# Norm between two blocks of a Trainium2 kernel: the row factor through a matrix of ones

## The chip, the cores and the metric

The kernel runs on one core of one Trainium2 chip. The core has five engines with instruction queues of their own: TensorE (PE, matrix products into PSUM), VectorE (DVE), ScalarE (ACT, functions out of tables), GpSimd (POOL) and SyncE (SP, which here only starts transfers). They run at the same time and wait for each other through semaphores. The metric is the device time of one execution in microseconds (us); lower is better.

## What is computed

The reference runs two transformer blocks one after the other on 256 rows of 2048 columns, all in fp32. The first block normalises its input, runs a sliding-window attention with sinks, gates it, multiplies by `w_out_a`, and adds the normalised product to its input. The second block normalises that sum and goes on with two attention branches and a feed-forward part. What matters here is the seam:

```python
y = (o * silu(z)) @ w_out_a                 # (256, 2048)
x = x + rmsnorm(y, g_post)                  # end of the first block
h = rmsnorm(x, attn_norm_g_2)               # start of the second
proj = h @ w_in_2
# rmsnorm(y, g) = y * rsqrt(mean(y*y over the 2048 columns) + 1e-6) * g
```

So each of the 256 rows of y needs one factor, the reciprocal root of the mean of its squares. No row of x can be had before the last column of y is known.

## The kernel before

**Layout.** In this part the kernel holds everything transposed: a tile has 128 of the 2048 columns of the model in its partitions and the 256 rows of the sequence along its free axis. Sixteen such tiles make y. A sum over the model's columns is therefore a sum over partitions and over sixteen tiles, and the factor that comes out must stand as a row of 256 numbers in every partition, to be multiplied with the tiles.

**Products.** A product with weights is made of three parts in reduced fp32 (`F32R`): each weight is split by ACT into a high part `w_hi` (line 85) and by DVE into the rest `w_lo` (line 86), and the activations likewise (`split_scaled`, lines 248 and 249). All matrix products are issued by the helper `mm`, line 209. Products of plain fp32, as those with the tile `ones` (a 128x128 matrix of ones, line 215), show up as two passes each in the trace.

**The stage around the change.** The loop at line 663 makes blocks 0 to 14 of `out_a`. For each, `total` adds two halves of a PSUM bank (ACT copy line 417, DVE add line 212) into a half of a tile `y`, `sq.add` squares it (ACT, line 265) and adds the square to the accumulator `sq.acc` (DVE, line 212), and line 667 scales `y` by the gain. Block 15 is made by `gemm_sum` (line 358), which sums all three parts into one PSUM region; its square (`sq.last`) is taken from PSUM and kept apart from the accumulator (`urgent=True`).

Then follows the norm. `sq.sums` (line 271) takes both squares, 128 rows of the sequence at a time, as the stationary operand against one column of `ones`: four products that give the 256 sums as two columns of 128 partitions. `rstd` (line 281) makes the mean plus epsilon on DVE (line 285) and raises it to the power -0.5 on POOL (line 290, exponent tile `mhalf`). `rows` (line 293) puts the 256 factors on two diagonals (DVE, line 297) and multiplies them by `ones`, which gives the row of factors in every partition, in PSUM. `residual_1` (line 688) multiplies a tile of y by that row (line 691) and adds x (line 692); `second_h` (line 695) splits the result for the next products, `in_2`. Both are issued tile by tile as `in_2` asks for them.

**What sets the order.** The program is written with a tile framework. Each engine works through its instructions in a fixed order, which a planner decides when the kernel is built, from its own estimates of when each input is ready; the order of the code only decides between instructions that are ready. Instructions marked by `pin` (in `residual_1` and `second_h`) keep the order of the code among each other. Tiles come from pools with a fixed number of slots (`unit`: 57 tiles of 128x512; PSUM banks with tag `t`: two), and an instruction that writes a new tile waits for a free slot.

`busy(n, cols)` (line 352) issues n products of the first gated tile with itself, of which nobody reads the result. They take up PE between real products.

**ACT's tables.** A function of ACT needs its table loaded. Before the change the trace has three loads, at lines 232, 1055 (Silu) and 1110 (Sqrt, at the end).

Of the kernel before, what the change touches and what calls it, by code (L numbers as in the profile page):

```python
# [9 lines left out]
F32 = mybir.dt.float32  # L10
F32R = mybir.dt.float32r
AF = mybir.ActivationFunctionType
ALU = mybir.AluOpType

P = 128
S = 256
D = 2048
# [3 lines left out]
EPS = 1e-6  # L21
# [150 lines left out]
def block_kernel(ctx, tc, order, w, x01, xt, bc, rw, cst, out):  # L172
    nc = tc.nc
    const = ctx.enter_context(tc.tile_pool(name="const", bufs=1))
# [12 lines left out]
    def unit(name, dt=F32):  # L187
        return up.tile([P, 512], dt, name=name, tag="u", bufs=NU)
# [7 lines left out]
    def sm(name, n=4):  # L196
        return small.tile([P, n], F32, name=name, tag="sm", bufs=16)

    def bank(tag):
        return psum.tile([P, 512], F32, name=f"ps_{tag}", tag=tag, bufs={"g": 4, "s": 2, "t": 2}[tag])  # L200

    def half(t, i):
        return t[:, (i % 2) * S:(i % 2) * S + S]
# [4 lines left out]
    def mm(o, a, b, start, stop):  # L208
        nc.tensor.matmul(out=o, lhsT=a, rhs=b, start=start, stop=stop, skip_group_check=True)  # L209
# [5 lines left out]
    ones = const.tile([P, P], F32, name="ones")  # L215
# [12 lines left out]
    warm = psum.tile([P, 512], F32, name="ps_warm", tag="t", bufs=2)  # L228
    for i in range(13):
        nc.tensor.matmul(out=warm[:, 0:P], lhsT=ones, rhs=ones, start=True, stop=True, skip_group_check=True)  # L230
    mhalf = const.tile([P, 4], F32, name="mhalf")
    nc.scalar.activation(out=mhalf, in_=ones[:, 0:4], func=AF.Copy, scale=-0.5)
    ident = const.tile([P, P], F32, name="ident")
# [3 lines left out]
    def gcol(base, i):  # L237
        return colt[:, base + i:base + i + 1]
# [42 lines left out]
    def rstd(src, dim, scale=None):  # L281
        n = src.shape[-1]
        t = sm("ms", n)
        if scale is None:
            nc.vector.tensor_scalar(out=t, in0=src, scalar1=1.0 / dim, scalar2=EPS, op0=ALU.mult, op1=ALU.add)  # L285
        else:
            nc.vector.scalar_tensor_tensor(out=t, in0=src, scalar=1.0 / dim, in1=scale, op0=ALU.mult, op1=ALU.mult)
            nc.vector.tensor_scalar(out=t, in0=t, scalar1=EPS, scalar2=None, op0=ALU.add)
        r = sm("rstd", n)
        nc.gpsimd.tensor_tensor(out=r, in0=t, in1=mhalf[:, 0:n], op=ALU.pow)  # L290
        return r

    def rows(r, rb=None):

        dg = unit("diag")[:, 0:S]
        for tb in range(2):
            nc.vector.tensor_scalar(out=dg[:, tb * P:tb * P + P], in0=ident, scalar1=r[:, tb:tb + 1], scalar2=None,
                                    op0=ALU.mult)
        ps = bank("t")
        mm(ps[:, 0:S], ones, dg, True, True)  # L300
        if rb is not None:
            nc.vector.tensor_copy(out=rb, in_=ps[:, 0:S])
        return ps[:, 0:S]
# [48 lines left out]
    def busy(n, cols):  # L352

        ps = bank("s")
        for _ in range(n):
            mm(ps[:, 0:cols], g[0][:, 0:P], g[0][:, 0:cols], True, True)

    def gemm_sum(name, m, acts):

        kind[0] = "hi"  # L360
        ps = bank("g")
        n = len(acts)
        for k in range(n):
            hi, lo = W.take(name, k * P, m * P)
            mm(ps[:, 0:S], hi, acts[k][:, 0:S], k == 0, False)
            mm(ps[:, 0:S], hi, acts[k][:, S:], False, False)
            mm(ps[:, 0:S], lo, acts[k][:, 0:S], False, k == n - 1)
            between.tiles(1)
        return ps

    def blocks(name, m0, n, acts):

        for j, ps in enumerate(gemm4(name, range(m0, m0 + 4), acts)):
            yield j, ps
        for j in range(4, n):
            yield j, gemm(name, m0 + j, acts)
# [38 lines left out]
    def total(o, ps):  # L415

        nc.scalar.copy(out=o, in_=ps[:, S:])
        tt(o, o, ps[:, 0:S], ALU.add)
# [75 lines left out]
    sq = Squares(8)  # L494
# [30 lines left out]
    rb = unit("rb_a")[:, 0:S]  # L525
# [134 lines left out]
    sq = Squares(16, urgent=True)  # L660
    y2 = [unit("y") for _ in range(8)]
    n_next = len(W.order) + KD * KD
    for m, ps in blocks("out_a", 0, 15, g):
        t = half(y2[m // 2], m)
        total(t, ps)
        sq.add(t)
        nc.scalar.activation(out=t, in_=t, func=AF.Copy, scale=gcol(G_POST, m))
        y.append(t)
        if m in (5, 8, 11):
            W.cut(len(W.order))  # L670
            W.cut(len(W.order) + HALF)
            for i in range(2):
                W.cut(n_next + (m - 5) // 3 * CH + i * HALF,
                      [(unit("w_hi_u", F32R), unit("w_lo_u", F32R)) for _ in range(2)])
    ps = gemm_sum("out_a", 15, g)
    sq.add(ps[:, 0:S])
    sums = sq.sums()
    busy(8, P)
    r = rstd(sums, D)
    busy(2, S)  # L680
    rb = rows(r)
    busy(8, 512)
    t = half(y2[7], 1)
    nc.scalar.activation(out=t, in_=ps[:, 0:S], func=AF.Copy, scale=gcol(G_POST, 15))
# [143 lines left out]
    for u in range(4):  # L828
# [12 lines left out]
        for tb in range(2):  # L841
            t = unit("v_m")
# [162 lines left out]
    for i in range(4):  # L1005
        parts = []
        for tb, ps in enumerate(gemm_nat("diff", i * 512, y_d)):
            t = gates[i][tb]
# [67 lines left out]
    for cb in range(3):  # L1076
        for tb, ps in enumerate(gemm_nat("down", cb * 512, act)):
            residual(cb, tb, ps)
            t = x2n[2 * cb + tb]
# [18 lines left out]
    for tb in range(2):  # L1098
# [3 lines left out]
        for i, (cols, ps) in enumerate(parts):  # L1102
# [3 lines left out]
            if i + 1 < len(parts):  # L1106
                nc.vector.scalar_tensor_tensor(out=ms3[:, tb:tb + 1], in0=tot[:, 5 * tb + 3:5 * tb + 4],
                                               scalar=1.0 / D, in1=ms3[:, tb:tb + 1], op0=ALU.mult, op1=ALU.add)
        r = sm("rms", 1)
        nc.scalar.activation(out=r, in_=tot[:, 5 * tb + 2 + len(parts):5 * tb + 3 + len(parts)], func=AF.Sqrt,  # L1110
                             scale=1.0 / D, bias=ms3[:, tb:tb + 1])
        nc.vector.reciprocal(out=r, in_=r)  # L1112
        for cb in range(4):
            t = x2n[2 * cb + tb]
# [110 lines left out]
```

## Time and profile before

| | us |
|---|---|
| median of 3 runs | 1979.8 (1979.0 to 1981.18) |
| the profiled execution, its own time | 1978.53 |
| its span, first to last instruction | 1976.8 |
| last product of block 15 issued | 329.14 |
| squares of block 15 start on ACT | 329.46 |
| first `y` times the row factor on DVE | 332.88 |
| first product of `in_2` | 335.00 |

The times inside the execution count from the start of its span. [...] A name as `ps_t<-ones,sq` reads: the tile written, then the tiles read. PE is the execution of products, PEld the load of their stationary operand. The times of single products are modelled at their ends.

### The profile page before, as it was taken

What the parts mean: (1) busy time and instruction counts of PE and PEld (TensorE: products, weight loads), DVE (VectorE), ACT (ScalarE), POOL (GpSimd) and SP (SyncE); (2) the same over time, 40 slices, a digit from 0 to 9 for tenths busy, and PEclk for the clock granted to TensorE, in tenths of its full rate; (3) what the DMA queues carried; (4) which work ended last, traced back from release to release, by engine and by line L of the source; (5) the groups of instructions that cost most, each with busy time, mean ns of one, the idle gap of its engine ahead of it and who ended that gap; (6) DMA issues with size and microseconds to landing.
All of it is one profiled execution on the core that took longest, in us unless ns stands there. A gap on an engine that the chain in (4) does not pass through costs nothing. (4 is left out here: it accounts for less than half of the span.)

```text
span 1976.8 us, 27209 instructions
## 1 busy us (share of the span) xinstructions
PE 1961.3 (99%) x9756; PEld 1648.6 (83%) x9756; DVE 1246.6 (63%) x1960; ACT 1000.3 (51%) x1580; POOL 524.8 (27%) x1067
## 2 busy tenths in 40 slices
PE   9999999999999999999999999999999999999998
PEld 8888888888888888888888888887888888888887
DVE  7889766888856655566666666655555555545553
ACT  6677664755645444455554444544444444444443
POOL 0555200022401300013143575433444333330000
PEclk9999999999999999999999999999999999999999
DMA  8565554455555555555556665655656556565553
GB/s 304 186 210 192 187 208 164 171 177 175 174 187 195 173 220 226 198 182 181 204 202 228 212 216 186 241 204 199 207 206 206 204 208 210 206 226 192 192 191 107
DMA packets 100793, 393.16 MB, mean 199 GB/s; under 512 B 27248, under 2 KB 53104, under 8 KB 57520
## 3 DMA queue, kind: packets, MB, share of 16 engines
q1 hardware_dynamic: 65184, 366.17, 52.1%
q0 software_dynamic: 34320, 23.27, 4.2%
q10 hardware_dynamic: 1152, 1.97, 0.3%
q8 instruction: 77, 1.26, 0.3%
q14 instruction: 60, 0.49, 0.1%
HBM read 364.03 MB, written 2.10 MB: 185 GB/s over the span
## 5 line engine op out<-in xcount | busy, mean ns | idle before, releaser
L86 DVE TENSOR_TENSOR w_lo<-w_raw,w_hi 128x1024 fp32r<-128x1024 f32 (+1 forms) x677 | 820.8, 1217 | 555.6 <-ACT w_hi L85 550.7
L85 ACT CAST w_hi<-w_raw 128x1024 fp32r<-128x1024 f32 (+1 forms) x677 | 706.6, 1048 | 699.4 <-PE ps_g L209 632.1
L209 PE MATMUL ps_g<-w_lo,t_hi 128*128 128x512 f32 x1176 | 457.6, 389 | 0.8 <-DVE w_lo L86 0.8
L209 PE MATMUL ps_g<-w_hi,t_hi 128*128 128x512 f32 x1176 | 457.6, 389 | 0.3 <-ACT w_hi L85 0.3
L209 PE MATMUL ps_g<-w_hi,t_lo 128*128 128x512 f32 x1176 | 457.3, 389 | 0.0
L452 POOL DMA_DIRECT2D turned<-turn x576 | 281.7, 497 | 393.2 <-DVE turn L459 169.6
L209 PE MATMUL ps_g<-h,w_hi 128*128 128x512 f32 x1160 | 283.7, 393 | 1.9 <-ACT w_hi L85 1.8
L452 POOL DMA_DIRECT2D prob_t<-prob_tr x336 | 164.5, 498 | 400.6 <-DVE prob_tr L467 249.6
L209 PEld LDWEIGHTS ps_g<-w_lo,t_hi 128*128 128x128 f32 x1176 | 220.7, 188 | 47.0 <-DVE w_lo L86 1.1
L209 PEld LDWEIGHTS ps_g<-w_hi,t_hi 128*128 128x128 f32 x1176 | 220.7, 188 | 46.7 <-ACT w_hi L85 0.7
L209 PEld LDWEIGHTS ps_g<-w_hi,t_lo 128*128 128x128 f32 x1176 | 220.7, 188 | 45.6
L209 PEld LDWEIGHTS ps_g<-h,w_hi 128*128 128x128 f32 x1160 | 212.0, 188 | 46.6 <-issue 2.7
L209 PE MATMUL ps_g<-w_hi,h 128*128 128x512 f32 x768 | 240.9, 391 | 0.0
L209 PEld LDWEIGHTS ps_g<-w_hi,h 128*128 128x128 f32 x768 | 144.2, 188 | 29.8
L209 PEld LDWEIGHTS ps_g<-h,w_lo 128*128 128x128 f32 x1160 | 150.2, 191 | 9.9 <-issue 3.0
L209 PE MATMUL ps_g<-h,w_lo 128*128 128x256 f32 x1160 | 155.1, 284 | 0.0
L209 PE MATMUL ps_g<-w_lo,h 128*128 128x512 f32 x384 | 149.7, 390 | 0.8 <-DVE w_lo L86 0.8
L290 POOL TENSOR_TENSOR rstd<-ms,mhalf 128x2 f32<-128x2 f32 (+1 forms) x10 | 8.4, 837 | 354.5 <-DVE ms L285 338.8
L209 PEld LDWEIGHTS ps_g<-w_lo,h 128*128 128x128 f32 x384 | 72.1, 188 | 16.2 <-DVE w_lo L86 1.6
L452 POOL DMA_DIRECT2D o_t<-o_tr x128 | 62.8, 498 | 63.5 <-issue 24.9
L209 PE MATMUL ps_g<-w_hi,y_m 128*128 128x512 f32 x256 | 79.5, 389 | 0.0
L209 PE MATMUL ps_g<-w_hi,y_d 128*128 128x512 f32 x256 | 79.0, 389 | 0.0
(242 smaller groups left out, 1800.8 us busy)
## 6 DMA issues: line engine op xcount, KB each, us to landing
w_raw<-w SPq DMA_DIRECT2D x337, 1024.0 KB, 5.0
turned<-turn POOLq DMA_DIRECT2D x576, 16.0 KB, 3.9
prob_t<-prob_tr POOLq DMA_DIRECT2D x336, 24.0 KB, 3.6
row<-rw POOLq DMA_DIRECT2D x12, 256.0 KB, 4.0
prob_t<-prob_tr SPq DMA_DIRECT2D x112, 24.0 KB, 2.9
w_raw<-w SPq DMA_DIRECT2D x5, 512.0 KB, 7.5
x1n<-turn SPq DMA_DIRECT2D x128, 16.0 KB, 1.8
o_t<-o_tr POOLq DMA_DIRECT2D x128, 16.0 KB, 3.9
```

What stands on the lines that cost most here:

```text
L85: a = nc.scalar.copy(out=hi[:, q], in_=src[:, q])
L86: b = nc.vector.tensor_tensor(out=lo[:, q], in0=src[:, q], in1=hi.bitcast(F32)[:, q], op=ALU.subtract)
L209: nc.tensor.matmul(out=o, lhsT=a, rhs=b, start=start, stop=stop, skip_group_check=True)
L290: nc.gpsimd.tensor_tensor(out=r, in0=t, in1=mhalf[:, 0:n], op=ALU.pow)
L452: (fourth if fourth and a == 3 else queue).dma_start(out=o[32 * b:32 * b + 32, a * n:a * n + n], in_=tr[32 * a:32 * a + 32, b * n:b * n + n])
```

## The change

The row factor is made in another way. The product takes the matrix of ones as the stationary operand and the squares as the moving one, 256 columns wide, so each product gives the sums as a row in every partition at once: one for the accumulated squares of blocks 0 to 14, written ahead of block 15's products, and one for block 15's own squares behind them, into the same PSUM region. ACT then takes the root of sums / 2048 + epsilon into an SBUF tile `rb_y`, with epsilon from a new tile of one column, and DVE takes the reciprocal of all 256 columns in place. The mean on DVE, the power on POOL, the two diagonals and the second product with ones go away here (`sums`, `rstd` and `rows` stay for the other norms). Between the two products of ones, a Sqrt of the accumulated squares into `rb_y` is written, whose result is overwritten later. The fillers behind the norm become `busy(4, P)` and `busy(8, 512)`, where they were `busy(8, P)`, `busy(2, S)` and `busy(8, 512)`.

```diff
@@ -228,6 +228,8 @@
     for i in range(13):
         nc.tensor.matmul(out=warm[:, 0:P], lhsT=ones, rhs=ones, start=True, stop=True, skip_group_check=True)
+    eps = const.tile([P, 1], F32, name="eps")
+    nc.vector.memset(eps, EPS)
     mhalf = const.tile([P, 4], F32, name="mhalf")
@@ -672,13 +674,17 @@
+    rb = unit("rb_y")[:, 0:S]
+    sums = bank("t")[:, 0:S]
+    mm(sums, ones, sq.acc, True, False)
+    nc.scalar.activation(out=rb, in_=sq.acc, func=AF.Sqrt)
     ps = gemm_sum("out_a", 15, g)
     sq.add(ps[:, 0:S])
-    sums = sq.sums()
-    busy(8, P)
-    r = rstd(sums, D)
-    busy(2, S)
-    rb = rows(r)
+    mm(sums, ones, sq.last, False, True)
+    busy(4, P)
+    nc.scalar.activation(out=rb, in_=sums, func=AF.Sqrt, scale=1.0 / D, bias=eps)
+    nc.vector.reciprocal(out=rb, in_=rb)
     busy(8, 512)
     t = half(y2[7], 1)
     nc.scalar.activation(out=t, in_=ps[:, 0:S], func=AF.Copy, scale=gcol(G_POST, 15))
```

## The prediction

> **What bounds the kernel now.** I began with the profile's page, which has TensorE (PE) at work for 99% of the span, so anything that holds PE up goes into the total.
>
> ```profile
> span 1976.8 us, 27209 instructions
> PE 1961.3 (99%) x9756; PEld 1648.6 (83%) x9756; DVE 1246.6 (63%) x1960; ACT 1000.3 (51%) x1580; POOL 524.8 (27%) x1067
> ```
>
> Next I took the busy time in the stretch of the norm and in the one behind it (columns: stretch, its length, busy time of PE, weight load, DVE, ACT and POOL, granted clock).
>
> ```profile
> 329.50:335.00 5.50, 4.54 (x27) 3.61 (x26) 2.69 (x9) 1.63 (x4) 0.71 (x1) 1.00 0.27 85
> 335.00:360.00 25.00, 25.00 (x143) 21.96 (x144) 23.33 (x49) 13.35 (x23) 0.00 (x0) 1.00 0.22 85
> ```
>
> From 335.00 us PE has no free time, so a later start there is not made up again. In the norm PE looks busy (4.54 of 5.50 us), but its own timeline shows with what: everything called ps_s is filler from busy(), whose result nobody reads. (Columns: start, duration, engine, line, what; in brackets the idle time before it.)
>
> ```profile
> 329.14 0.28 PE L209 MATMUL ps_g<-g,w_lo 128*128 128x256 f32 x1
> 329.26 0.50 PE L209 MATMUL ps_t<-ones,sq 128*128 128x1 f32 x4
> 329.62 0.42 PE L209 MATMUL ps_s<-g 128*128 128x128 f32 x2
> 329.90 0.61 PE L209 MATMUL ps_t<-ones,sq 128*128 128x1 f32 x4
> 330.36 1.15 PE L209 MATMUL ps_s<-g 128*128 128x128 f32 x8
> 332.14 0.70 PE L209 MATMUL ps_t<-diag,ones 128*128 128x256 f32 x2 [0.63 <-DVE diag L297]
> 332.49 2.18 PE L209 MATMUL ps_s<-g 128*128 128x512 f32 x8
> 335.00 0.50 PE L209 MATMUL ps_g<-h,w_hi_u 128*128 128x512 f32 x1 [0.34 <-DVE h L249]
> ```
>
> So the real limit is the chain from the last product of block 15 (its end is 329.14 + 0.28 = 329.42) to the first product of the next stage at 335.00. The timelines of DVE and of ACT fill it in.
>
> ```profile
> 324.11 0.42 DVE L212 TENSOR_TENSOR y<-y,ps_g 128x256 f32<-128x256 f32 x1 [3.06 <-ACT y L417]
> 325.02 0.42 DVE L212 TENSOR_TENSOR sq<-sq 128x256 f32<-128x256 f32 x1 [0.48 <-ACT sq L265]
> 330.54 0.16 DVE L285 TENSOR_SCALAR ms<-ps_t 128x2 f32<-128x2 f32 x1 [5.10 <-PE ps_t L209]
> 331.61 0.48 DVE L297 TENSOR_SCALAR diag<-ident,rstd 128x128 f32<-128x128 f32 x2 [0.91 <-POOL rstd L290]
> 332.88 0.42 DVE L691 TENSOR_TENSOR y<-y,ps_t 128x256 f32<-128x256 f32 x1 [0.79 <-PE ps_t L209]
> 333.34 0.42 DVE L692 TENSOR_TENSOR y<-y,x01t 128x256 f32<-128x256 f32 x1
> ```
>
> ```profile
> 323.71 0.37 ACT L417 COPY y<-ps_g 128x256 f32<-128x256 f32 x1 [3.39 <-PE ps_g L209]
> 324.57 0.42 ACT L265 ACTIVATE sq<-y 128x256 f32<-128x256 f32 x1 [0.49 <-DVE y L212]
> 325.02 0.51 ACT L667 ACTIVATE y<-y,x01t 128x256 f32<-128x256 f32 x1
> 329.46 0.38 ACT L265 ACTIVATE sq<-ps_g 128x256 f32<-128x256 f32 x1 [3.93 <-PE ps_g L209]
> ```
>
> The chain runs: squares of block 15 on ACT 329.46 to 329.84, their sums on PE from 329.90, mean on DVE at 330.54, power on POOL, two diagonals on DVE at 331.61, product with ones on PE at 332.14, first multiplication of y by the row on DVE at 332.88. From the squares to that multiplication it is 332.88 - 329.46 = 3.42 us, and from it to PE's start 335.00 - 332.88 = 2.12 us, a part that the change leaves alone.
>
> **The change part by part.** Removed, on the path: the mean, the power, the diagonals and the second product, 332.88 - 330.54 = 2.34 us with their hand-overs, and four passes of a one-column sum. Added on the path: two passes of ones against 256 columns, Sqrt of 256 columns on ACT, and Reciprocal of 256 columns on DVE. Off the path: a product of ones with the accumulated squares, an early Sqrt, and a memset of one column.
>
> The product first. In a busy PE a pair of fp32 passes over 256 columns looks so, in two stretches of PE's timeline:
>
> ```profile
> 395.81 0.67 PE L209 MATMUL ps_t<-diag,ones 128*128 128x256 f32 x2
> 396.13 0.58 PE L209 MATMUL ps_g<-h,w_hi 128*128 128x512 f32 x1
> ```
>
> ```profile
> 398.18 0.59 PE L209 MATMUL ps_t<-diag,ones 128*128 128x256 f32 x2
> 398.42 0.58 PE L209 MATMUL ps_g<-c,w_hi 128*128 128x512 f32 x1
> ```
>
> A pair gives its result after 0.59 to 0.70 us and holds PE's issue for 0.24 to 0.32 us. On the path I take 0.60, off it 0.28.
>
> Sqrt has 128x256 out of PSUM with a per-partition operand. The nearest row among ACT's groups:
>
> ```profile
> L542 ACT ACTIVATE v_a<-ps_s,r_a 128x256 f32<-128x256 f32 x2 | 0.9, 488 | 0.0
> ```
>
> I take 0.49 us; the squares without that operand took 0.38, the lower bound.
>
> Reciprocal is the large unknown, since the kernel before has it only on 1 and 4 columns (minimum/median/maximum ns, from the answers for those two lines). Below it, from DVE's groups, are additions at two widths.
>
> ```profile
> L571 DVE RECIPROCAL rec<-rec x16: 168/176/180, 52.2 to 206.3; 128x4 f32<-128x4 f32 x16
> L1112 DVE RECIPROCAL rms<-rms x2: 151/158/164, 1966.1 to 1969.9; 128x1 f32<-128x1 f32 x2
> ```
>
> ```profile
> L212 DVE TENSOR_TENSOR sq<-sq 128x256 f32<-128x256 f32 x38 | 15.8, 421 | 1.9 <-ACT sq L265 1.0
> L212 DVE TENSOR_TENSOR sq<-sq 128x512 f32<-128x512 f32 x7 | 4.8, 687 | 0.3
> ```
>
> Three more columns cost 176 - 158 = 18 ns, 6 ns each; an addition costs (687 - 421) / 256 = 1.04 ns each. So Reciprocal seems to take about six steps per column, and 158 + 255 x 6 ns = 1.69 us. The ends: if it went like an addition, 0.42 us; with the widest pair of these rows, (180 - 151) / 3 = 9.7 ns a column, 151 + 255 x 9.7 = 2.62 us. I take 1.69 because it comes from the same instruction, though stretched sixty-fold.
>
> [...]
>
> The new path, from the start of the squares: squares 0.38, hand-over to PE 329.90 - 329.84 = 0.06, pair of passes 0.60, hand-over to ACT 329.46 - 329.42 = 0.04, Sqrt 0.49, hand-over to DVE 324.11 - (323.71 + 0.37) = 0.03, Reciprocal 1.69, next DVE instruction 333.34 - (332.88 + 0.42) = 0.04. Sum 3.33 us against 3.42: 0.1 us shorter. The gain from the removed steps goes into Reciprocal almost whole.
>
> Two things move the start. The product of ones with the accumulated squares stands in the code ahead of block 15's products, where its four passes used to stand behind them, in the shadow of the squares on ACT (329.46 to 329.84). Its input is ready only at 325.02 + 0.42 = 325.44, while block 15's products run from about 323.6. The planner orders PE by readiness: before, it put two fillers ahead of the sums of the last squares, which the code has first. So I expect the pair inside block 15, where it pushes the end back by 0.28 us. Bounds: nothing if it lands behind the products; if it stands at their head, PE waits 325.44 - 323.7 = 1.7 us for it, with all of block 15 queued behind. Second, PE has only fillers in the 0.42 us between its last product and the last squares, since the accumulated sums are gone from there. Four of 128 columns at (1.15 - 0.28) / 7 = 0.12 us fill 0.5, and the planner may add one of 512 at about 0.25; the last sums would then start some 0.1 us late (0 to 0.25). Sum: -0.1 + 0.28 + 0.1 = +0.3 us.
>
> Costed at nothing: the memset, in DVE's wait for the first load; residual_1 reading its factor from SBUF instead of PSUM (the addition rows above are of SBUF at 0.42, L691 reads PSUM at 0.42); the slot that the factor now holds until the last residual_1, because the slots of block 15's inputs come free as its products run; and the two changes of activation table, of which the next rows tell (ACT's timeline at the end of the kernel, and one row of the stage at 424 us).
>
> ```profile
> 1964.39 1.28 ACT L1110 ACT_TABLE_LOAD   x1
> 1965.68 0.29 ACT L1110 ACTIVATE rms<-tot,ms 128x1 f32<-128x1 f32 x1
> 1966.20 0.42 ACT L1073 ACTIVATE sqn<-x1n 128x256 f32<-128x256 f32 x1 [0.22 <-DVE x1n L1071]
> ...
> 1969.61 0.29 ACT L1110 ACTIVATE rms<-tot,ms 128x1 f32<-128x1 f32 x1
> ```
>
> ```profile
> 424.08 0.49 ACT L442 ACTIVATE prob<-prob,negmax,neg_r 128x128 f32<-128x128 f32 x1 [3.55 <-DVE negmax L212]
> ```
>
> A load costs 1.28 us. Squares run between two Sqrts with no load between, so after the early Sqrt the squares and the second Sqrt need none. The early load and Sqrt (1.28 + 0.49 = 1.77 us) fall from 325.53 on into the 3.93 us in which ACT waits for block 15. The load back to Exp falls into the 3.55 us ahead of the first Exp behind the norm. Uncovered, each is 1.28 us.
>
> **The rivals.** *A, Reciprocal as fast as an addition*: for it speaks that its 4 columns take hardly longer than other small instructions; against it the slope. Then 1.69 - 0.42 = 1.27 us less: -1.0 us, 1978.8.
>
> *B, PE held at the head of block 15* by the moved product, because PE works in order and the planner took its input to be ready early: 1.7 us and the sums themselves. For it speaks the place in the code, against it that in the 25 us behind the norm, where the planner mixes several sums, PE never waited. +1.8 us with the rest as forecast, 1981.6.
>
> *C, slower through the clock.* The fillers shrink by six, and none is left to bridge Reciprocal: from about 330.55, where the last sums have been issued, seven of 512 columns at 2.18 / 8 = 0.27 us end near 332.5, and the next stage starts near 335.3. PE rests 2.8 us, where its longest rest here was 0.63. The end of the kernel shows what a rest does (PE's timeline, then the stretches):
>
> ```profile
> 1968.24 0.28 PE L209 MATMUL ps_s<-w_hi,t_lo 128*128 128x256 f32 x1
> ```
>
> ```profile
> 1971.00:1972.00 1.00, 0.00 (x0) 0.00 (x0) 0.29 (x1) 0.47 (x1) 0.00 (x0) 0.68 0.53 199
> 1972.00:1976.80 4.80, 0.00 (x0) 0.00 (x0) 0.00 (x0) 0.00 (x0) 0.00 (x0) 0.50 0.53 179
> ```
>
> [...] If it falls, the products behind the norm run at half rate until it rises. The trace has no product at the low level, so the price is half of the low stretch; taking the 5.4 us that it lasted there, 2.7 us: +3.0, 1982.8. It is slower by over 0.2% from about 7.5 us at the low level on. For it speaks that measured fall, against it that PE works hard right up to and after the rest.
>
> *D, the tables uncovered*: 2 x 1.28 = 2.6 us, +2.9 and 1982.7, if both loads waited for the input of their activation. Only ACT's idle rows speak against it. [...]
>
> **How the numbers follow.** The profiled execution took 1978.53 us beside its span of 1976.8; the median of the runs shown is 1979.8. The sum of +0.3 us makes 1978.8 of the one and 1980.1 of the other, which I forecast. Chances: the forecast 0.68, A 0.08, B 0.07, C 0.10, D 0.03, and 0.04 that the planner, given other instructions, orders something far from here differently by microseconds. A measurement tells about 0.2%, 4 us, from no change. The forecast, A, B, and the usual C and D all lie inside it: 0.88 for no difference; 0.08 slower (a long C, a D that also holds up the stage at 424 us, half of the planner's share); 0.04 faster. The range takes A below and C above with the spread of the runs (1979.0 to 1981.18): 1978.2 to 1983.0.
>
> **What would show it.** In the changed profile: Reciprocal on 128x256 near 1.7 us, Sqrt near 0.49 right before it; a pair ps_t<-ones,sq on 256 columns among block 15's products with no idle time before it; L691 for the first time 3.2 to 3.5 us after the squares of block 15; the first product of the next stage 2.1 us later, about 0.3 us past 335.00, with an idle time of 2 to 3 us before it and the granted clock at 1.00 behind it; two more table loads in ACT's idle time. A Reciprocal far from 1.7 us, an idle PE inside block 15, or a granted clock under 1.00 from 333 us on would make the prediction wrong, as would a difference of over 1 us that arises elsewhere.

## The result, and the profile after

The changed kernel takes 1985.67 us, median of 8 executions (1981.34 to 1987.64); the kernel before took 1979.59 in the 8 executions beside them (1978.44 to 1982.5). The ratio on record is 1.0023, with a 95% interval of 1.0014 to 1.0032: slower by little but clear of noise, and above the range of the prediction. (The ratios on record are not quotients of the medians; that would be 1.0031 here.) A second set gave 1.0021 (1.0012 to 1.003).

The profiled execution is the quickest of the eight, 1981.34 us, which is 2.8 us more than the profiled one of before (1978.53). So there are two things to find: these 2.8 us, which a profile can show, and why most executions took 4 us more than that one.

First the page of the kernel after: the span, the engines, and of the transfers the queue q8, which carries instructions.

```profile
span 1979.6 us, 27197 instructions
...
PE 1960.6 (99%) x9744; PEld 1647.7 (83%) x9744; DVE 1247.7 (63%) x1959; ACT 1004.2 (51%) x1584; POOL 524.3 (26%) x1066
...
q8 instruction: 77, 1.26, 0.3%
```

PE's work fell by 0.7 us and its span grew by 2.8: the difference is idle time. PE has 12 products fewer than before (9756). Now the stage of the norm, by PE's timeline of the kernel after:

```profile
325.11 0.28 PE L209 MATMUL ps_g<-g,w_hi 128*128 128x256 f32 x1
325.31 0.70 PE L209 MATMUL ps_t<-sq,ones 128*128 128x256 f32 x2
325.66 0.47 PE L209 MATMUL ps_g<-g,w_hi 128*128 128x256 f32 x1
325.96 0.28 PE L209 MATMUL ps_g<-g,w_lo 128*128 128x256 f32 x1
...
329.55 0.28 PE L209 MATMUL ps_g<-g,w_lo 128*128 128x256 f32 x1
329.67 0.45 PE L209 MATMUL ps_s<-g 128*128 128x128 f32 x3
330.31 0.70 PE L209 MATMUL ps_t<-sq,ones 128*128 128x256 f32 x2 [0.19 <-ACT sq L267]
330.66 2.31 PE L209 MATMUL ps_s<-g 128*128 128x128 f32 x9
335.46 0.50 PE L209 MATMUL ps_g<-h,w_hi_u 128*128 128x512 f32 x1 [2.50 <-DVE h L251]
```

The timelines of ACT and of DVE in the same kernel:

```profile
325.36 1.28 ACT L681 ACT_TABLE_LOAD   x1
326.65 0.42 ACT L681 ACTIVATE rb_y<-sq 128x256 f32<-128x256 f32 x1
329.87 0.38 ACT L267 ACTIVATE sq<-ps_g 128x256 f32<-128x256 f32 x1 [2.80 <-PE ps_g L209]
...
331.05 0.48 ACT L686 ACTIVATE rb_y<-ps_t,eps 128x256 f32<-128x256 f32 x1 [0.43 <-PE ps_t L209]
```

```profile
331.55 1.75 DVE L687 RECIPROCAL rb_y<-rb_y 128x256 f32<-128x256 f32 x1 [6.30 <-ACT rb_y L686]
333.34 0.42 DVE L697 TENSOR_TENSOR y<-y,rb_y 128x256 f32<-128x256 f32 x1
```

The chain is the forecast one: the pair for the accumulated squares inside block 15 and without idle time, the early load and Sqrt in ACT's wait, Sqrt 0.48, Reciprocal 1.75, the first multiplication 3.47 us behind the start of the squares. The first product of `in_2` stands at 335.46 in place of 335.00. This execution started its first stages 0.19 us earlier than the one of before (the same product of the stage ahead of the norm is at 297.30 there and at 297.49 before), so the norm costs 0.65 us more. Almost all of it is the pair inside block 15. The products there follow each other at 0.12 us; from the one ahead of the pair to the second one behind it, 325.11 to 325.96, it is 0.85 us in place of 2 x 0.12, so the pair costs PE 0.61 us. In the same way block 15's last product stands at 329.55 against 329.14, which is 0.60 us later with the start taken off, and the chain from the squares to the first multiplication is 0.05 us longer. The stretches of the norm and behind it show the granted clock, the share of PE's full clock that the trace has as granted, at 1.00 in both:

```profile
329.70:335.50 5.80, 3.11 (x17) 2.23 (x15) 3.84 (x7) 2.18 (x5) 0.00 (x0) 1.00 0.27 81
335.50:360.50 25.00, 25.00 (x140) 21.64 (x141) 22.55 (x49) 12.96 (x22) 0.00 (x0) 1.00 0.23 85
```

To find the rest of the 2.8 us I took the start of the same product, counted from the start of the span, in both traces: the difference is 0.46 us at the head of `in_2`, 0.79 from 392 us on, 1.23 at 771, 1.37 from 1065 to 1360, 2.81 at 1407, and 2.81 to the end. Most of it arises outside the norm, and 1.44 us at one place, a thousand us later. PE's timelines there, before and after:

```profile
1365.76 0.50 PE L209 MATMUL ps_g<-w_hi,t_hi 128*128 128x512 f32 x1 [0.32 <-ACT w_hi L85]
```

```profile
1368.57 0.49 PE L209 MATMUL ps_g<-w_hi,t_hi 128*128 128x512 f32 x1 [1.77 <-ACT w_hi L85]
```

The program is the same there; PE waits 1.77 us for a cast where it waited 0.32.

### The profile page after: what moved, and what is told of

Read it like the earlier page. It is cut to its first block, busy times and chain, and to the rows that moved or that the text cites. A ratio compares the mean times of both kernels' runs of the same rounds, so it can differ in the third digit from the quotient of the medians.

```text
span 1979.6 us, 27197 instructions
## 1 busy us (share of the span) xinstructions
PE 1960.6 (99%) x9744; PEld 1647.7 (83%) x9744; DVE 1247.7 (63%) x1959; ACT 1004.2 (51%) x1584; POOL 524.3 (26%) x1066
```

## The experiments

Every comparison is with the kernel before, run on the same chip beside it; its medians there were 1979.89, 1980.53, 1980.64 and 1979.93 us. The theories after the result were these. *Clock*: the rest of 2.5 us in front of `in_2` lets the granted clock fall in most executions, and a fall costs some us. *Elsewhere*: the shorter stream of PE changes something far from the norm. *Sum*: the new path itself costs more than one profile shows.

### The changed kernel again

> The changed kernel unaltered, to see an execution as slow as its median. Clock theory (the 2.5 us in which TensorE rests before the next stage let the granted clock fall in most executions): the mean granted clock of most executions is 0.996 to 0.998, and a profile with such a mean shows 0.50 for 6 to 10 us soon after 335 us, with 512-column products spaced about 0.45 us there instead of 0.23; the time is about 1985.5 then, and about 1981 in an execution whose mean is 0.999. Path theory (the 6 us come from the longer chain of the norm and from waits further down, such as the later landing of the transposed tiles near 1366 us): the clock is 1.00 up to the end in every profile, and the time is spread over waits of TensorE.

Median 1984.87 (1981.24 to 1987.14, 10 executions), ratio 1.0021 (1.0012 to 1.003). This time the profile fell on a long execution, 1987.14 us with a mean granted clock of 0.996 (0.999 in the first profile). Its stage of the norm is the same within 0.01 us (rest of 2.51, granted clock 1.00). The clock fell at two other places. Stretches of this run, cut where the granted clock changes:

```profile
778.80:781.47 2.67, 0.65 (x3) 0.56 (x4) 0.67 (x1) 1.75 (x2) 0.00 (x0) 1.00 1.02 433
781.47:784.88 3.41, 3.41 (x12) 2.83 (x11) 3.28 (x5) 2.70 (x5) 0.00 (x0) 0.50 1.00 423
784.88:788.29 3.41, 3.41 (x22) 3.05 (x21) 2.57 (x3) 0.90 (x2) 0.00 (x0) 1.00 1.02 406
...
1371.98:1378.80 6.82, 6.09 (x14) 4.78 (x15) 4.08 (x4) 3.25 (x4) 0.00 (x0) 0.50 0.72 274
1378.80:1385.60 6.80, 6.80 (x31) 5.61 (x30) 3.15 (x3) 2.17 (x3) 0.00 (x0) 1.00 0.51 188
```

And what PE did ahead of each, in its timeline:

```profile
780.82 1.97 PE L209 MATMUL ps_g<-h,w_hi 128*128 128x512 f32 x5 [2.03 <-ACT w_hi L85]
...
1371.45 0.50 PE L209 MATMUL ps_g<-w_hi,t_hi 128*128 128x512 f32 x1 [2.13 <-ACT w_hi L85]
```

In 3.41 us at 0.50 PE issued 12 products, in the next 3.41 us at 1.00 it issued 22: ten products, 10 x 3.41 / 22 = 1.55 us, were lost. In the longer stretch it was 14 in 6.09 busy us against 31 in 6.80: 6.09 - 14 x 6.80 / 31 = 3.0 us. With the longer waits (2.03 against 1.76 and 2.13 against 1.77, 0.6 us together) and a start 0.65 us later this makes 5.8 us, which is 1987.14 - 1981.34; what is left, 0.3 us more near 739 us and 0.5 less near 1024, is small. So this long execution is explained in the main by falls of the clock, and they came behind rests outside the norm, one of them the very wait that the change had made longer. The other long executions have no profile, but their mean granted clocks. Of the 18 executions of both sets only 3 have a mean granted clock of 0.999 (1981.24 to 1981.45 us), the others 0.996 to 0.998 (1982.85 to 1987.64); of the kernel before, 47 of the 106 executions that stand beside the runs of this section have 0.999. (Every profile has the clock at 0.50 in its last 3.3 to 5.7 us, 5.4 in that of before and 4.1 in the first of after, behind PE's last product, which alone leaves a mean of 0.999; 3.41 us more make it 0.998. By the means the number of falls can only be estimated.)

### Fill the rest; take the fillers away before; fill it without losing instructions

```diff
 after_fill18 (on the kernel after)      after_18x256 (on the kernel after)
-    busy(8, 512)                       -    busy(8, 512)
+    busy(18, 512)                      +    busy(18, S)

 before_no_fill (on the kernel before)
-    busy(8, 512)
```

`busy(18, 512)` covers Reciprocal, and it also gives PE ten products more. `busy(18, S)` issues as many products of half the width (256 columns), so PE has the count of instructions of the first and about the rest of the unchanged fillers.

> The changed kernel with 18 instead of 8 fillers of 512 columns, so that TensorE has something to do until the first product of the next stage near 335.4 us; nothing else is ordered otherwise. Clock theory: mean granted clock 0.999 in every execution, and 1979.9 to 1981 us, that is 0.3 to 1 us over the kernel before. Path theory: 1984 to 1987, as the changed kernel.

> The kernel before without its eight fillers of 512 columns behind the norm: TensorE rests 0.6 us before the product of the diagonals and about 2.2 us behind it, the chain of the norm is unchanged. Clock theory: the granted clock falls in a good part of the executions, mean 0.996 to 0.998 there, and the median is 2 to 5 us over the kernel before. Path theory: no difference, within 1 us.

> The changed kernel with its eight fillers of 512 columns replaced by 18 of 256, which take as long (0.12 us each against 0.26), so that TensorE rests 2.5 us before the next stage as in the changed kernel, but executes 10 products more, nearly as many as the kernel before. Fetch theory (with 12 product instructions less, TensorE's instruction packet near 1360 us comes about 3 us later relative to the program, falls into a load of weights and holds up the transposed tile that TensorE waits for near 1367 us): that wait is 0.3 to 0.6 us again instead of 1.8 to 2.1, undisturbed executions take 1979.9 to 1980.5 instead of 1981.3, the median is 1980.5 to 1982. Theory that only the rest in the norm and its clock count: as the changed kernel, 1984.5 to 1986.

The 18 fillers gave 1980.77 (1980.0 to 1984.41), ratio 1.0007 (0.9998 to 1.0016): 4 us of the 5 to 6 are back, and 6 of 11 executions have a mean clock of 0.999. The kernel before without fillers gave 1981.89 (1980.35 to 1987.19), 1.0012 (1.0003 to 1.0021), with no execution of 0.999 among ten. In its profile the clock fell in the norm itself, at the end of a rest of 2.25 us, as it did in the kernel with 18 narrow fillers behind one of 2.21. PE's timeline and the stretch of the first, then the stretches of the second:

```profile
335.29 0.77 PE L209 MATMUL ps_g<-h,w_hi_u 128*128 128x512 f32 x1 [2.25 <-DVE h L249]
```

```profile
335.06:338.47 3.41, 3.18 (x11) 2.84 (x12) 3.31 (x10) 1.37 (x4) 0.00 (x0) 0.50 0.00 0
```

```profile
333.80:336.13 2.33, 0.15 (x1) 0.15 (x2) 2.23 (x7) 1.01 (x2) 0.00 (x0) 1.00 0.00 0
336.13:339.54 3.41, 3.41 (x13) 3.03 (x14) 3.31 (x10) 1.43 (x3) 0.00 (x0) 0.50 0.00 0
```

That is rival C at its place: 3.41 us low, and `in_2`'s products behind it 1.5 us later than in the kernel before (1.55 later than with 18 wide fillers in the other case), with the starts of the executions taken off. So the clock can fall at a rest there; the two profiles of the changed kernel itself show none at that place.

But the narrow fillers, with nearly the same rest as the changed kernel, came out at 1982.81 (1980.0 to 1985.19), 1.0009 (1.0 to 1.0018), better than the changed kernel, though above the 1980.5 to 1982 that was expected. They differ from it in ten more PE instructions, and at 1369 us PE's wait is as short as before the change:

```profile
1368.99 0.49 PE L209 MATMUL ps_g<-w_hi,t_hi 128*128 128x512 f32 x1 [0.26 <-ACT w_hi L85]
```

### Take instructions away elsewhere

```diff
 before_warm7 (on the kernel before)     fill18_warm8 (on after, with busy(18, 512))
-    for i in range(13):                -    for i in range(13):
+    for i in range(7):                 +    for i in range(8):
```

The warm-up products at the head of the program (line 229) are taken as a place to change the count: nobody reads their result, and each is two of the products that the page counts. The first kernel has 12 fewer than before, and both have as many as the changed kernel (9744).

> The kernel before with 7 instead of 13 products of ones at its very start, which are 12 product instructions less, as many as the change takes away; nothing else is different, the norm least of all. Fetch theory: the instruction packet near 1357 us comes at 1360 or later, TensorE waits 1.5 to 2.1 us near 1366 us instead of 0.3, undisturbed executions take 1979.6 to 1980.2 instead of 1978.4, and the median is 1 to 4 us over the kernel before. Theory of the norm's rest alone: as the kernel before, up to a start that may differ by 1 us either way.

> The changed kernel with 18 fillers of 512 columns (no rest in the norm) and 8 instead of 13 products of ones at the start, so that it has exactly the changed kernel's number of products. Fetch theory: the wait near 1367 us is 1.5 to 2.1 us, undisturbed executions take about 1981.3 where the same kernel with 13 products at the start took 1980.0 to 1980.8, and the median is 1981.5 to 1984. Theory of the norm's rest alone: 1980 to 1981 as with 13.

Both start later: with the shorter warm-up PE rests 1.88 us at the head in the first and 1.32 in the second, and its products of 256 columns take 0.41 us there up to 9 us, in place of 0.28. The product at the head of `in_2` is 1.07 us later than before in the one, 0.79 later than with 18 fillers and the full warm-up in the other. The wait is there in both, though neither has the rest in the norm. PE's timeline of the first, then of the second:

```profile
1367.39 0.51 PE L209 MATMUL ps_g<-w_hi,t_hi 128*128 128x512 f32 x1 [1.31 <-ACT w_hi L85]
```

```profile
1371.27 0.50 PE L209 MATMUL ps_g<-w_hi,t_hi 128*128 128x512 f32 x1 [1.64 <-ACT w_hi L85]
```

Their medians are 1982.57 (ten executions, without one of 3291.92 us with a mean clock of 0.556; 1.001, 1.0 to 1.0019) and 1982.88 (1.0014, 1.0005 to 1.0023), and in both profiles the clock falls to 0.50 for 3.41 us at that wait, from 1368.57 and from 1372.0. In the second it had fallen once before, from 781.49, behind a rest of 1.94 us.

The wait's other end is a transfer beside a weight load. Queue q8 carries instructions, 77 packets of 16 KB; by their times I take them to be PE's. In the trace of the kernel after, PE starts 204 to 286 products and loads of their operands from one packet to the next, 253 in the mean (212 to 282 and 253 before), while DVE starts 10 to 56 instructions. A stream that is 12 products shorter, if so, should get each later packet at a later point of the program; the table below shows that for the one near 1360 us. There that point lies by a transfer of 1 MB of weights (queue q1), which is issued while a transposed tile (`turned`) is on its way. First the kernel before: the issue on SP, the packets of q8 in the stretch 1357.00 to 1357.95, and ACT's wait for the tile.

```profile
1357.95 0.33 SPq L54 DMA_DIRECT2D w_raw<-w  x1
```

```profile
q8 instruction: 1, 0.02, 6.3%
```

```profile
1362.98 0.62 ACT L480 CAST t_hi<-turned 128x512 fp32r<-128x512 f32 x1 [5.56 <-DMA turned<-turn]
```

Then the kernel after, q1 and q8 in the stretch 1361.50 to 1363.50:

```profile
1359.44 0.33 SPq L54 DMA_DIRECT2D w_raw<-w  x1
```

```profile
q1 hardware_dynamic: 104, 0.85, 102.4%
q8 instruction: 1, 0.02, 2.9%
```

```profile
1365.80 0.62 ACT L482 CAST t_hi<-turned 128x512 fp32r<-128x512 f32 x1 [6.87 <-DMA turned<-turn]
```

How long the pieces of the tile took to land, by its transfers before and after:

```profile
DMA to landing us min/median/max: 2.2/3.0/4.8
```

```profile
DMA to landing us min/median/max: 1.6/1.6/6.2
```

Before, the packet is on its way ahead of the load's issue; after, it comes 2.7 us behind it, in the middle of the load. The slowest piece of the tile is the last one, issued 0.16 us behind the load in both; it lands after 6.2 us in place of 4.8, ACT's cast waits 6.87 us for it against 5.56, and the casts of the weights, which stand behind it in ACT's order, hold up PE. Over all profiles of this study (start of the packet less issue of the load, from the trace's transfers; PE's wait in the row near 1368):

| kernel | PE products | packet less load, us | slowest piece, us | PE waits, us |
|---|---|---|---|---|
| before | 9756 | -0.75 | 4.8 | 0.32 |
| before, no fillers | 9748 | -0.11 | 4.9 | 0.52 |
| after, 18 fillers | 9754 | -0.05 | 4.8 | 0.34 |
| after, 18 narrow fillers | 9754 | -0.01 | 4.6 | 0.26 |
| the six other kernels told below | 9754 to 9762 | -5.0 to -0.06 | 4.8 to 4.9 | 0.41 to 0.65 |
| before, 7 warm-up products | 9744 | +0.54 | 5.5 | 1.31 |
| 18 fillers, 8 warm-up products | 9744 | +1.03 | 5.9 | 1.64 |
| after, first profile | 9744 | +2.69 | 6.2 | 1.77 |
| after, second profile | 9744 | +2.75 | 6.3 | 2.13 |

Whatever was edited, the four profiles with 9744 products wait 1.3 to 2.1 us and the ten with more wait 0.26 to 0.65. That the count of PE's instructions makes the wait is shown, in both directions. That the packet does it, by holding up the last piece of the tile beside the load, is what the order of the columns suggests; the packet was not moved by itself. In the times the count shows less clearly than in the traces: the intervals of the changed kernel and of the one with 18 narrow fillers overlap, so do those of 18 fillers with 8 and with 13 warm-up products, and that of 7 warm-up products reaches down to 1.0.

### The pieces of the change

```diff
 before_sqrt2 (on the kernel before)
+    eps = const.tile([P, 1], F32, name="eps")
+    nc.vector.memset(eps, EPS)
...
+    nc.scalar.activation(out=sm("early", 2), in_=sq.acc[:, 0:2], func=AF.Sqrt)
...
-    r = rstd(sums, D)
+    r = sm("rstd_y", 2)
+    nc.scalar.activation(out=r, in_=sums, func=AF.Sqrt, scale=1.0 / D, bias=eps)
+    nc.vector.reciprocal(out=r, in_=r)
```

The old layout, with the factor made by ACT and DVE on two columns and no POOL.

> The kernel before with only the root exchanged: the two columns of sums go to ACT's Sqrt (mean and epsilon as its scale and bias, table loaded early in ACT's idle time) and DVE's Reciprocal of 2 columns, in place of the mean on DVE and the power on POOL; sums, diagonals, rows and all fillers as before. Path theory as well as clock theory: Sqrt 0.29 and Reciprocal 0.16 us in place of 330.54 to 331.61, so the first product of the next stage comes 0.4 to 0.6 us earlier, the clock stays at 1.00, and the time is 1979.0 to 1979.5. If the change of tables alone cost something, or the other order of a few products that it brings with it near 395 us, it would be slower than before by 1 us or more.

Median 1981.24 (1978.19 to 1982.82), 1.35 us above the kernel before beside it, but by the ratio, 1.0 (0.9991 to 1.0009), no difference. DVE's timeline and PE's:

```profile
331.00 0.17 DVE L684 RECIPROCAL rstd_y<-rstd_y 128x2 f32<-128x2 f32 x1 [5.39 <-ACT rstd_y L683]
```

```profile
334.67 0.50 PE L209 MATMUL ps_g<-h,w_hi_u 128*128 128x512 f32 x1 [0.32 <-DVE h L251]
...
738.85 0.50 PE L209 MATMUL ps_g<-w_hi,h 128*128 128x512 f32 x1 [1.28 <-ACT w_hi L85]
```

The stage is 0.50 us shorter (335.00 - 334.67, and this execution started 0.17 us later). Reciprocal on 2 columns takes 0.17 us, on 256 it takes 1.75: that width is what the changed kernel pays for having no second product. In this execution the gain was given back at 738.85, where PE waits 1.28 us for a cast for which it did not wait in the profile of before.

```diff
 fill_no_early (on after, with busy(18, 512))
-    nc.scalar.activation(out=rb, in_=sq.acc, func=AF.Sqrt)
```

> The changed kernel with 18 fillers of 512 columns and without the early Sqrt of the accumulated squares, so that ACT loads its table between the squares of block 15 and the Sqrt that the norm needs. If a load costs 1.28 us and runs on while ACT waits for the sums, Sqrt starts 0.5 to 0.95 us later than with the early one and so does the first product of the next stage; the two other places near 424 us and in the stage behind do not change. If the load started only with the sums, it would be 1.28 us.

ACT's timeline of this kernel, then PE's of it and of the kernel with 18 fillers and the early Sqrt:

```profile
331.05 1.28 ACT L685 ACT_TABLE_LOAD   x1
...
332.34 0.47 ACT L685 ACTIVATE rb_y<-ps_t,eps 128x256 f32<-128x256 f32 x1
```

```profile
336.77 0.50 PE L209 MATMUL ps_g<-h,w_hi_u 128*128 128x512 f32 x1 [1.12 <-DVE h L251]
```

```profile
335.88 0.50 PE L209 MATMUL ps_g<-h,w_hi_u 128*128 128x512 f32 x1 [0.23 <-DVE h L251]
```

Without the early Sqrt the load falls between the squares and the Sqrt, and `in_2` starts 0.89 us later, less than the load's 1.28, since ACT would have waited for the sums in part of it. Sqrt follows the load at 332.34 - (331.05 + 1.28) = 0.01 us, so the load itself took its 1.28 us and no more here. Median 1984.17 (1981.79 to 1986.41), 1.0015 (1.0005 to 1.0025), which is more than 0.89 us can make. The profiled execution is 4.66 us longer than that with the early Sqrt, and 4.0 us of it arise near 742 us: PE waits 1.92 us for a cast at 741.88, and the clock is at 0.50 for 3.41 us from 744.38 on. So the times of this pair do not give the price of the load; the rows of the norm do.

```diff
 fill_acc_late (on after, with busy(18, 512))
-    mm(sums, ones, sq.acc, True, False)
     nc.scalar.activation(out=rb, in_=sq.acc, func=AF.Sqrt)
     ps = gemm_sum("out_a", 15, g)
+    mm(sums, ones, sq.acc, True, False)
     sq.add(ps[:, 0:S])
```

> The changed kernel with 18 fillers of 512 columns and with the product of ones and the accumulated squares moved behind block 15, where ACT squares that block's result anyway. By the prediction's step the pair cost 0.28 us inside block 15: the first product of the next stage comes 0.2 to 0.35 us earlier than with the pair inside. If the sums of the last squares now queue behind the pair and the fillers, a part of it, up to 0.15 us, is lost again. The median of the runs cannot tell this apart; the timeline can.

PE's timeline:

```profile
329.09 0.28 PE L209 MATMUL ps_g<-g,w_lo 128*128 128x256 f32 x1
329.21 0.59 PE L209 MATMUL ps_t<-sq,ones 128*128 128x256 f32 x2
...
329.84 0.70 PE L209 MATMUL ps_t<-sq,ones 128*128 128x256 f32 x2
330.19 4.82 PE L209 MATMUL ps_s<-g 128*128 128x128 f32 x21
335.01 0.50 PE L209 MATMUL ps_g<-h,w_hi_u 128*128 128x512 f32 x1
```

Back in the shadow of the squares, the pair costs nothing: `in_2` starts at 335.01, and 0.60 us earlier than with 18 fillers once the start of the execution (0.27 earlier) is taken off. That is what the pair costs inside block 15 by the rows above (0.61), and more than the 0.2 to 0.35 that was expected. Median 1980.27 (1979.01 to 1984.02, 8 executions), ratio 1.0 (0.9989 to 1.001).

### In search of a version that beats both

```diff
 before_f778, sqrt2_f778, acc_late_f778 (on before, before_sqrt2, fill_acc_late)
+                if (u, c, i) == (1, 0, 1):
+                    busy(6, 512)
                 ps = gemm("dqk", c + 4 * u + i, h)
```

Six fillers in the rest at 778 us, behind which the clock had fallen in two profiles.

> The kernel before with six fillers of 512 columns ahead of the second product block of the differential branch's second round, where TensorE rests 1.8 us near 778 us for a late load of weights; the norm is untouched. If rests of about 2 us are what lets the granted clock fall in a part of the executions, this rest shrinks to 0.2 to 0.4 us, fewer executions show a mean clock of 0.998, and the median falls by 0.5 to 1.5 us to 1978.4 to 1979.5, below both kernels. If the clock's part in the spread of the executions is elsewhere, nothing changes beyond 0.3 us.

> The kernel before with two edits: the root by ACT and the reciprocal by DVE on the two columns of the sums (in place of mean and power), and six fillers ahead of the second product of dqk's block at 778 us. It asks whether the half microsecond that the short form gains in the norm (first product of in_2 0.47 us earlier, measured) shows in the time once a later rest of PE is shortened. Theory (what the time loses between executions comes from falls of the granted clock behind rests of about 2 us): the gain stays, the rest near 778 is 0.9 us in place of 1.8, the median comes out 0.5 to 1.0 us under the kernel before, a ratio of 0.9995 to 0.9997. Rival (a gain of half a microsecond moves the later instructions against the transfers and is given back at another rest, as at 739 us before): median equal to or above the kernel before, and a rest near 739 us of over 1.5 us in the profile.

> The changed kernel with 18 fillers of 512 columns, the product with the accumulated squares behind block 15's products, and six fillers ahead of the second product of dqk's block at 778 us. Theory: the stage of the norm costs what it cost before (first product of in_2 within 0.1 us of the kernel before, counted from the products behind it), so the median lies within 0.7 us of the kernel before, a ratio of 0.9997 to 1.0004, and the wait of PE near 1368 us stays under 0.7 us, since more fillers only bring PE's instructions earlier to the transfers. Rival (the whole product on 256 columns costs more than the stage shows): 1.0008 or more, with the added time in the first 30 us behind the norm.

On the kernel before the rest shrank from 1.77 us to 0.91 (0.2 to 0.4 was expected), and the time did not: 1981.16 (1978.44 to 1983.22), 1.0003 (0.9994 to 1.0012). In that profile the clock fell in the norm of before, unchanged here, behind the idle 0.63 us that the prediction had taken as harmless; PE's timeline, then the stretch at the low clock:

```profile
332.25 1.12 PE L209 MATMUL ps_t<-diag,ones 128*128 128x256 f32 x2 [0.63 <-DVE diag L297]
```

```profile
332.39:335.80 3.41, 3.41 (x9) 2.64 (x10) 2.32 (x6) 1.01 (x2) 0.00 (x0) 0.50 0.00 0
```

The root on two columns with these fillers gave 1980.67 (1978.36 to 1983.23), 1.0003 (0.9993 to 1.0012). Its profile has waits of 1.01 and 0.76 us near 739, and the clock at 0.50 from 740.38 on for 3.41 us. That is near the rival's reading, half a microsecond gained in the norm and given back at another wait, though the rival had named one wait of over 1.5 us, and the interval of the ratio holds both readings. The third gave 1980.52 (1979.45 to 1985.44), 1.0002 (0.9992 to 1.0012), with a wait of 0.53 us near 1369, and the first product of `in_2` 0.05 us later than before, counted from the start of the stage ahead: as the theory had it, no loss and no gain in the norm. Its profiled execution, 1982.67 us without a fall of the clock, has a wait of 1.60 us at 740.01. None of the versions beats the kernel before by what can be measured.

The waits near 740 us deserve a look of their own, since the count does not sort them. In four kernels (the root on two columns, with and without the fillers at 778 us; 18 fillers without the early Sqrt; the third one above) PE waits 1.01 to 1.92 us there, in the ten other profiles at most 0.76; all four have 9754 products or more. In the four, the first of the weight loads there lands 6.0 to 6.7 us after its issue, in the ten after 4.9 to 5.2. In three of the four a packet of q8 starts 1.0 to 3.3 us behind that load's issue, in the ten others 4.5 us or more; that fits a packet in a load, as near 1368. The fourth, which waits longest, has it at 4.6 us. So what a packet does to a load stays open.

## Why the prediction was wrong

The time, 1980.1 us in a range of 1978.2 to 1983.0, was too low by 5.6 us, and the chance of 0.88 for no difference went to the wrong case.

*The sum of the stage* was right in its path and too small by 0.35 us. It said +0.3 us; measured 0.65.

| step | forecast, us | measured, us |
|---|---|---|
| pair on the path | 0.60 | 0.70 |
| hand-over from there to Sqrt | 0.04 | 0.04 |
| Sqrt | 0.49 | 0.48 |
| Reciprocal | 1.69 | 1.75 |
| squares to first multiplication | 3.33 | 3.47 |
| last sums late | 0.1 | 0: 0.06 behind the squares, as before |
| pair inside block 15 | 0.28 | 0.60, both by the end of block 15 and by moving the pair back |

The mis-sized term is the pair. Its 0.28 us was the issue of the pair alone; the fence that it came from has the product behind the first pair at 0.58 us, where one of 512 columns takes 0.39 elsewhere in the page of before, so the pair slows its neighbours as well.

The stretch of Reciprocal from 4 columns to 256 came within 0.06 us, and rival A falls: 1.75 us is far from an addition's 0.42. Rival B falls: PE did not wait at the head of block 15. Rival D falls too: the early load stands in ACT's idle time, the load back to Exp at 421.33 in the wait ahead of the first Exp (of which 2.25 us are left), and what the early one would cost uncovered is 0.89 us, not 1.28.

*The clock was the step that was mis-sized*, rival C. The prediction saw the rest (2.8 us forecast, 2.50 measured) and had the price of one fall nearly right (2.7 us for one low stretch; measured 1.55 for 3.41 us and 3.0 for 6.82). The end of the kernel, from which it took that price, has the clock at 0.50 from 1971.36 us on, 2.84 us behind PE's last product; in the first profile of after the fall came 4.12 us behind it. The prediction failed in taking the granted clock as one outcome, 1.00 or 0.50, the same in every execution, with a chance of 0.10 for the second. The runs show that it falls in some executions and not in others of the same kernel, the one before included as its mean clocks and the profile with its norm unchanged tell, and more often in the changed kernel: 15 of its 18 executions have a mean under 0.999, 59 of 106 of the kernel before. A median holds the expected price of such falls, and the one profile of before, with a mean of 0.999, showed none of them. Of the kernel before, the median stands 1.1 us above the profiled execution (1979.59 and 1978.53), of the one after 4.3 us (1985.67 and 1981.34). That difference of 3.3 us goes with the clock: executions with a mean of 0.999 take 1981.24 to 1981.45 us after and 1978.96 in the median before, so without falls only some 2.4 us stand between the kernels. Where it fell in the changed kernel, as far as a profile shows it, was not the norm, for which rival C had it, but 781 and 1372 us.

*What was costed at nothing and was not*: the shorter stream of PE. The prediction counted what six fillers less leave open in the norm, and not that these and six passes of the norm's own products, 12 in all, change something in the rest of the program. That is the wait at 1368 us: 1.45 us and more directly, in both profiles of the changed kernel, and a rest of 2 us, behind which the clock fell in the second (2.13 us). "A difference of over 1 us that arises elsewhere" was named as what would make it wrong; the nearest chance, 0.04, was for another order of instructions, and the order there is unchanged.

*How much each made.* The profiled executions, both without a fall, differ by 2.81 us: -0.19 from the start, 0.65 in the norm, 0.33 behind it (products in another order from 354 to 360 us), 0.44 near 739 us, 0.14 near 1024, 1.44 near 1368. By ratios, restoring the instructions alone (18 narrow fillers) takes the changed kernel from 1.0021 to 1.0009, some 2.4 us; filling the rest as well takes it to 1.0007; moving the pair back, to 1.0. From the first to the last the intervals are apart (1.0012 to 1.003 and 0.9989 to 1.001), so all of it together takes the loss away; the intervals of single steps overlap, and what the rest in the norm costs by itself in the changed kernel is not settled; in the kernel before a rest of that size costs a ratio of 1.0012 (1.0003 to 1.0021). Open is also why the clock falls behind one rest of 2 us and not behind the next: the profiles have it fall after rests from 0.63 to 2.25 us, and not fall after 2.50 and 2.51.

## What to carry to other kernels

A profile is one execution: before costing a rest of PE at nothing because the granted clock stayed at 1.00 behind it, compare the profiled time and its mean clock with the other executions, and give the rest an expected price. Fillers and warm-up products are part of the layout of the program as well: where their number changes, look for waits that change far behind the edit, by following the same product through both traces. A wide elementwise operation that replaces a product has to be priced by its columns, since 256 columns of Reciprocal ate what a second product and two hand-overs had cost.

## What the runs showed of the hardware

- Reciprocal on DVE takes 1.75 us for 128x256, 0.17 for two columns and 0.18 for four: (1752 - 176) / 252 = 6.3 ns a column, where an addition takes 1.0.
- The granted clock fell to 0.50 for 3.41 us, once for 6.82, at rests of PE of 0.63 to 2.25 us, in some executions and not in others of the same kernel; 3.41 us at the low level cost 1.55 us.
- Instructions are transfers too: queue q8 moved 77 packets of 16 KB in this program, and with twelve products of PE fewer one of them came 2.7 us behind the issue of a weight load in place of 0.75 ahead; PE's wait near 1368 us grew by 1.45 us.
- A pair of plain fp32 passes on 256 columns cost PE 0.61 us among products in reduced fp32: 0.35 of issue, and 0.26 at the products around it.
- A load of an activation table took 1.28 us, with Sqrt 0.01 us behind it; 0.89 us of it lay on the path where the load began in ACT's wait.
